# Neighbourhood attention in a hybrid encoder layer: each column group's values loaded once and kept, and the first latent head loaded in two halves

## Chip, cores and metric

The kernel runs on one core of a Trainium2 chip. The metric is the device time of one execution in microseconds (us). The parts of the core are TensorE (PE in the tables; PEld is its weight load), VectorE (DVE), ScalarE (ACT), GpSimd (POOL), and SyncE (SP), from which every DMA of this kernel is issued, in one order that is fixed when the program is built. Sixteen DMA engines serve that one queue. 1 KB is 1024 bytes here, 1 MB is 10^6 bytes.

## The reference, cut to what matters

One encoder layer over 2048 tokens of width 1024. Its first half projects the normed input into three branches, norms each 64-wide group of the joined result and projects it back; its second half is a SwiGLU feed-forward. Two of the branches matter here.

```
# A: neighbourhood attention on a 32 x 64 token grid, 4 heads of 64 channels, window 8 rows x 16 columns
s = einsum('brqhd,brjwhd->bhrqjw', qg, k_band) * dh ** -0.5
s = where(col_ok, s + bias, -inf)
p = softmax(s over the window)
o = einsum('bhrqjw,brjwhd->brqhd', p, v_band)
# B: latent attention, 8 heads, keys of 64 + 32 channels, over all 2048 tokens
s = einsum('bqhd,bkhd->bhqk', q_nope, k_nope) + einsum('bqhr,bkr->bhqk', q_rope, k_rope)
o = einsum('bhqk,bkhd->bqhd', softmax(s * scale), v)
```

## The kernel before

Stages follow one another: the projections (which write queries, keys and values to DRAM scratch), the neighbourhood attention, the latent attention, the output projection, and the feed-forward. The change is in the neighbourhood attention and at its seam with the latent attention.

**Units.** The token grid is cut into four rows of units (r = 0 to 3, eight grid rows each) and four column groups (cg = 0 to 3, sixteen grid columns each). One such group, written (r,cg), has 128 queries; a unit is one head of a group, so there are 64 units, taken as r, then cg, then head h. The keys of group (r,cg) are the grid rows of `RWIN[r]` (11, 15, 15 and 12 rows) by the columns of `CWIN[cg]` (24, 32, 32 and 24 columns).

A unit goes through three steps. `scores` (L911): two matmuls of 264 to 480 columns into the bank `sp`, then on VectorE one instruction that adds the bias and takes the maximum (L922), on ScalarE the exponential (L925), and a scaling by the reciprocal sum, on VectorE for even heads and on GpSimd for odd ones (L928). `flip` (L935): three or four transposes on TensorE into `tp`, copied to `pt` by ScalarE. `values` (L949), for two heads at once: 12 or 16 matmuls of `pt` with the value tile into `op`, copied to `ot`; after the fourth column group `ot` is stored to `mixT` (L963). There are two banks each of `sp`, `tp` and `op`.

**Loads of a group.** `load_unit` (L889) is called while the group before it is at its second head. It loads the queries `nq` (two DMAs of 128 KB, three buffers), the values `nvt` (four DMAs, one for each grid row modulo four, three buffers), and, where the table is not there yet, the bias `bt` (one buffer for each kind of column group: left edge, middle, right edge). Values of overlapping row windows are loaded again in each row of units.

**The seam.** The last units share TensorE and VectorE with the first maximum steps of the latent attention (`max_step`, L848): sixteen of them, each two matmuls into `ps` from the tiles `qh` and `kh` of latent head 0, and a reduction of 1024 columns on VectorE (L857). A latent head has five tiles: `qh`, `ql`, `kh`, `kl` of 128 x 2048 floats, and `vt` of 128 x 16 x 64 floats, together 4.72 MB, filled by eleven DMAs of `load_head` (L817). The maxima and the first half of each score need `qh` and `kh`, the second half of a score `ql` and `kl`, and the sum over values `vt`. The heads have two pools, `hda` and `hdb`, used in turn.

**What sets the order.** Within the neighbourhood stage only SP's order is written by hand, and a DMA whose data or buffers are free early may be moved ahead; the other engines are ordered by the build's scheduler. From the latent attention on, all orders are by hand. `load_head(1)` is called at the third slot of the first latent unit (L1259); since the pool `hdb` is opened inside the neighbourhood stage, on the other side of memory, its buffers are free at once, and the scheduler puts its DMAs between the loads of groups (2,0) and (2,1). A DMA on SP waits until its buffer is free and until the DMA eight places before it has landed. What is behind it in SP's order waits too.

Of the kernel before, what the change touches and what calls it, by code (L numbers as in the profile page):

```python
# [13 lines left out]
F32 = mybir.dt.float32  # L14
F32R = mybir.dt.float32r
# [9 lines left out]
P = 128  # L25
T = 2048
# [5 lines left out]
HD = 64  # L32
NAH = 4
MH = 8
NOPE = 64
ROPE = 32
# [6 lines left out]
GW = 64  # L43
# [20 lines left out]
RWIN = [(0, 11), (4, 15), (12, 15), (20, 12)]  # L64
# [14 lines left out]
def encoder_trunk(ctx: ExitStack, tc: tile.TileContext, x, cols, pos, inv, rg, ind, sel, b_ada, w_ada, w_adat, crow, w_in, w_conv3,  # L79
# [731 lines left out]
    with ExitStack() as c3:  # L811
# [2 lines left out]
        hds = [mk3("hda", 1, side="right")]  # L814
        heads = {}

        def load_head(h):  # L817


            hd = hds[h % 2]  # L820
            q1 = hd.tile([P, T], F32R, name="qh")
            q2 = hd.tile([P, T], F32R, name="ql")
            k1 = hd.tile([P, T], F32R, name="kh")
            k2 = hd.tile([P, T], F32R, name="kl")
            vt = hd.tile([P, T // P, HD], F32, name="vt")
            ns, rs = slice(h * NOPE, (h + 1) * NOPE), slice(h * ROPE, (h + 1) * ROPE)
            for t, parts in ((q1, (qnh[ns], qrh[rs], qrl[rs])), (k1, (knh[ns], krh[:ROPE], krh[:ROPE])),
                             (q2, (qnh[ns], qnl[ns])), (k2, (knl[ns], knh[ns]))):
                r = 0
                for ap in parts:  # L830
                    n = ap.shape[0]
                    dma(t[r:r + n].bitcast(F32), ap)
                    r += n
            dma(vt, vd[:, h * HD:(h + 1) * HD].rearrange("(t p) d -> p t d", p=P))
            heads[h] = [q1, q2, k1, k2, vt, None]

        def load_rest(h, q3):

# [26 lines left out]
        with ExitStack() as c2:  # L865
# [1 line left out]
            nkp = [mk("nkh", 1), mk("nkl", 1)]  # L867
            nbp = mk("nbp", 1)
            nqp = mk("nqp", 3)
            nvp = mk("nvp", 3)  # L870
            nw = mk("nw", 3)
            nsm = mk("nsm", 6)
            nop = mk("nop", 1)
# [15 lines left out]
            def load_unit(r, cg):  # L889
                r0, nr = RWIN[r]  # L890
                c0, wc = CWIN[cg]
                nq = nqp.tile([P, NAH, P], F32R, name="nq")
                for e in range(2):
                    dma(nq[e * HD:(e + 1) * HD].bitcast(F32), heads_of((nqh, nql)[e], r * CH + cg * P, P))
                nqs[(r, cg)] = nq
                vt = nvp.tile([P, 4, NAH * HD], F32, name="nvt")
                rows = nvt.rearrange("(r q) d -> q r d", q=GW)[c0:c0 + wc]
                for e in range(4):
                    n = len(range(e, nr, 4))
                    dma(vt[e * wc:(e + 1) * wc, :n], rows[:, r0 + e:r0 + nr:4])  # L900
                vts[(r, cg)] = vt
                load_bias((RCAT[r], CCAT[cg]))

            def load_bias(key):
                if key not in bias:
# [43 lines left out]
            def values(r, cg, hp, pair):  # L949

                kt = kts(r, cg)
                op = pso.tile([P, CH], F32, name="op")
                for j, (o, n) in enumerate(kt):
                    for e, pt in enumerate(pair):
                        h = 2 * hp + e
                        pe.matmul(op[e * HD:(e + 1) * HD, :P], vts[(r, cg)][:n, j, h * HD:(h + 1) * HD], pt[:n, j],
                                  start=j == 0, stop=j == len(kt) - 1, skip_group_check=True)
                if cg == 0:
                    ots[hp] = nop.tile([P, CH], F32, name=f"ot{hp}")
                s.activation(ots[hp].rearrange("p (r q) -> p r q", q=GW)[:, :, cg * 16:(cg + 1) * 16],  # L960
                             op[:, :P].rearrange("p (r q) -> p r q", q=16), AF.Copy)
                if cg == 3:
                    dma(mixT[hp * P:(hp + 1) * P, r * CH:(r + 1) * CH], ots[hp])  # L963
# [6 lines left out]
            with tc.manual_schedule(engines={ET.SP}):  # L970
# [12 lines left out]
                for i in range(len(units) + S2):  # L983
                    if M0 <= i < M0 + 16:
                        u, j = mla[(i - M0) // 8], (i - M0) % 8
                        if j == 0:
                            mxs[u] = new_max()
                        max_step(*u, j, mxs[u])
                    if i < len(units):
                        r, cg, h = units[i]  # L990
                        with tc.issue_after(last_store[0].ins):
                            if h == 1 and 12 <= i + 4 < len(units):
                                load_unit(*units[i + 4][:2])
                            if (r, h) == (0, 0) and 1 <= cg < 3:
                                load_keys(1, cg + 1)
                            if (r, cg, h) == (2, 0, 0):
                                load_head(0)
                        prs[i] = scores(*units[i])
                    if 0 <= i - S1 < len(units):
                        pts[i - S1] = flip(*units[i - S1], prs.pop(i - S1))  # L1000
                    w = i - S2
                    if 0 <= w < len(units) and w % 2:
                        r, cg, h = units[w]
                        values(r, cg, h // 2, (pts.pop(w - 1), pts.pop(w)))
                hds.append(mk3("hdb", 1, side="right"))


        mk = mk3
        tTa = mk4("tTa", 1)
        small = mk4("small3", 4)  # L1010
# [942 lines left out]
```

## Time and profile before

| | us |
|---|---|
| median of 3 runs | 3072.84 (3072.07 to 3074.15) |
| the profiled execution, its own time | 3066.38 |
| span of its trace | 3064.6 |
| neighbourhood stage, first score matmul to first latent exponential | 634.0 to 789.1 |

A row of a timeline has the start, the duration, the engine, the line, the operation, what it writes and reads, and in brackets how long the engine was idle before it and who ended the wait. A row of windows gives, for each engine, its busy time and its instructions in the stretch, then the clock granted to TensorE as a share of full speed, the mean busy share of the DMA engines, and what they moved in GB/s. The stage is five per cent of the span; where an engine waits in it, the time of the whole program follows, since the stages around it depend on it.

### The profile page before, as it was taken

To read this page: it belongs to the slowest core of one execution; us is meant where nothing else is said; L and a number is where in the kernel's file an instruction comes from. 1 tells how busy PE (TensorE), PEld (TensorE's weight loads), DVE (VectorE), ACT (ScalarE), POOL (GpSimd) and SP (SyncE) were. 2 spreads that over 40 slices of the span, in tenths; PEclk is the share of its full clock that TensorE was granted. 3 is DMA by queue.
4 is the path that set the end of the run, shared out by engine and by line. 5 is a ranking of instruction groups with operands and counts; after the bars stand their busy time and mean duration, and the time that the engine had idled before them with its cause. 6 is when DMAs were issued, how large, how long until landed. Compare 5 with 4: busy or idle time off the path is not lost. (4 is left out here: it accounts for less than half of the span.)

```text
span 3064.6 us, 39020 instructions
## 1 busy us (share of the span) xinstructions
PE 2911.2 (95%) x13554; PEld 2159.4 (70%) x13554; DVE 1978.0 (65%) x2872; ACT 1305.8 (43%) x2302; POOL 1431.0 (47%) x1043
## 2 busy tenths in 40 slices
PE   6988999978999999999999899999999999999998
PEld 5877888855555555555477688788767788888887
DVE  7778684625566666666667865565576655555556
ACT  4544444545444444444546433333444333333443
POOL 4433333422477777766655644344353544443002
PEclk9999999978999999999999999999999999999999
DMA  6566656698243354540364434344566533333566
GB/s 220 174 225 217 213 169 176 199 224 186 57 119 100 99 136 116 131 99 13 97 219 164 131 114 131 105 135 147 169 200 227 184 104 103 103 103 101 190 222 224
DMA packets 333707, 463.00 MB, mean 151 GB/s; under 512 B 40499, under 2 KB 179683, under 8 KB 328965
## 3 DMA queue, kind: packets, MB, share of 16 engines
q1 hardware_dynamic: 333510, 460.52, 49.7%
q8 instruction: 106, 1.74, 0.2%
q14 instruction: 91, 0.75, 0.1%
HBM read 338.58 MB, written 117.51 MB: 149 GB/s over the span
## 5 line engine op out<-in xcount | busy, mean ns | idle before, releaser
L857 DVE TENSOR_REDUCE mx<-ps 128x1 f32<-128x1024 f32 x256 | 313.3, 1224 | 236.7 <-PE ps L856 236.5
L1361 DVE TENSOR_TENSOR whl<-draw,whl 128x512 fp32r<-128x512 f32 x372 | 311.3, 872 | 182.1 <-ACT whl L1360 181.7
L1230 ACT ACTIVATE p<-st 128x1024 f32<-128x1024 f32 x256 | 262.1, 1024 | 361.6 <-PE st L1223 271.3
L1360 ACT ACTIVATE whl<-draw 128x512 fp32r<-128x512 f32 x372 | 219.9, 625 | 307.6 <-PE bk L1466 214.0
L1237 POOL TENSOR_TENSOR acc<-acc,p 128x512 f32<-128x512 f32 x192 | 275.4, 1434 | 44.1 <-ACT p L1230 39.1
L1465 PE MATMUL bk<-whl 128*128 128x512 f32 x616 | 243.7, 396 | 18.2 <-DVE whl L1361 17.9
L1168 PE MATMUL op<-p,vt 128*64 128x512 f32 x1024 | 249.6, 608 | 0.0
L1464 PE MATMUL bk<-whl 128*128 128x512 f32 x616 | 240.8, 391 | 3.4 <-ACT whl L1360 3.4
L1466 PE MATMUL bk<-whl 128*128 128x512 f32 x616 | 240.5, 390 | 0.0
L1386 POOL TENSOR_TENSOR t<-draw 128x512 f32<-128x512 f32 x88 | 122.2, 1389 | 233.9 <-DMA draw<-in_w_gu 192.0
L1400 ACT ACTIVATE whl<-t 128x512 fp32r<-128x512 f32 x176 | 111.0, 631 | 278.2 <-PE bk L1682 236.1
L1680 PE MATMUL bk<-q,whl 128*128 128x512 f32 x528 | 209.0, 396 | 13.1 <-ACT ev L1687 8.8
L1681 PE MATMUL bk<-q,whl 128*128 128x512 f32 x528 | 207.3, 393 | 0.0
L1222 PE MATMUL st<-qh,kh 128*128 128x512 f32 x512 | 205.7, 402 | 1.2 <-ACT p L1230 1.2
L1682 PE MATMUL bk<-q,whl 128*128 128x512 f32 x528 | 206.7, 391 | 0.0
L1401 DVE TENSOR_TENSOR whl<-t,whl 128x512 fp32r<-128x512 f32 x176 | 164.4, 935 | 61.4 <-ACT whl L1400 56.9
L262 POOL TENSOR_TENSOR wlo<-raw,whi 128x768 fp32r<-128x768 f32 (+4 forms) x59 | 112.8, 1913 | 193.7 <-ACT whi L261 184.4
L1223 PE MATMUL st<-ql,kl 128*128 128x512 f32 x512 | 201.1, 393 | 0.0
L1386 POOL TENSOR_TENSOR t<-draw,t 128x512 f32<-128x512 f32 x88 | 118.4, 1346 | 137.0 <-DMA draw<-in_w_gu 117.5
L856 PE MATMUL ps<-kh,qh 96*128 96x512 f32 x512 | 176.5, 426 | 5.9 <-DMA kh<-krh 4.0
L320 PE MATMUL mm<-whi,hh 128*128 128x288 f32 (+3 forms) x512 | 170.2, 344 | 8.1 <-ACT hh L384 4.9
L856 PEld LDWEIGHTS ps<-kh,qh 96*128 96x128 f32 x512 | 87.1, 191 | 115.2 <-DVE acc L1238 79.5
(370 smaller groups left out, 7243.6 us busy)
## 6 DMA issues: line engine op xcount, KB each, us to landing
draw<-in_w_gu SPq DMA_DIRECT2D x176, 256.0 KB
draw<-actd SPq DMA_DIRECT2D x70, 512.0 KB
actd<-xs SPq DMA_DIRECT2D x88, 256.0 KB
draw<-wdt SPq DMA_DIRECT2D x40, 512.0 KB
actd<-ev SPq DMA_DIRECT2D x66, 256.0 KB
wt<-in_w_adat SPq DMA_DIRECT2D x32, 512.0 KB
draw<-in_w_out SPq DMA_DIRECT2D x32, 512.0 KB
draw<-in_w_down SPq DMA_DIRECT2D x30, 512.0 KB
```

The source lines that it names most:

```text
L856: pe.matmul(ps[:, e], qs, kh[:QKD, kc:kc + CH], start=True, stop=True)
L857: v.reduce_max(mx[:, t, i:i + 1], ps.rearrange("p a b -> p (a b)"), axis=AX.X)
L1168: pe.matmul(tl["op"][e * HD:(e + 1) * HD], vt[:, 2 * kp + e], tl["p"][kp][:, e], start=kp == 0, stop=kp == NP - 1, skip_group_check=True)
L1230: s.activation(p, st, AF.Exp, scale=SC)
L1237: g.tensor_tensor(out=acc[:, 0], in0=a[:, 0], in1=p[kp][:, 0], op=ALU.add)
L1360: s.activation(w[:, 0], raw[:, e], AF.Copy)
L1361: v.tensor_tensor(out=w[:, 1], in0=raw[:, e], in1=w[:, 0].bitcast(F32), op=ALU.subtract)
L1386: g.tensor_tensor(out=t, in0=a, in1=b, op=op)
L1464: pe.matmul(ps, th, wh, start=first, stop=False, skip_group_check=True)
L1465: pe.matmul(ps, th, wl, start=False, stop=False, skip_group_check=True)
L1466: pe.matmul(ps, tl, wh, start=False, stop=last, skip_group_check=True)
L1680: pe.matmul(ps, w[:, 0, k], th, start=first and k == 0, stop=False, skip_group_check=True)
```

## The change

The value tiles become four, one for each column group, each with all 32 grid rows (eight blocks of four), and are kept through the stage. `load_unit` fills blocks 0 to 2 of a group in the first row of units, blocks 3 to 7 in the second, and nothing in the third and fourth. The matmuls of `values` read block `RWIN[r][0] // 4 + j` instead of block j.

`load_head` gets a `parts` argument. Part 0 allocates all five tiles and loads `qh` and `kh`; part 1 loads `ql`, `kl` and `vt`. Head 0 is loaded as part 0 with unit (2,0,0), and as part 1 with unit (3,2,0). The pool `hdb` is opened after the neighbourhood stage's pools are closed, not before.

```diff
-        def load_head(h):
+        def load_head(h, parts=(0, 1)):
...
             hd = hds[h % 2]
+            if 0 in parts:
+                q1, q2, k1, k2 = [hd.tile([P, T], F32R, name=n) for n in ("qh", "ql", "kh", "kl")]
+                heads[h] = [q1, q2, k1, k2, hd.tile([P, T // P, HD], F32, name="vt"), None]
+                fill(q1, qnh[ns], qrh[rs], qrl[rs])
+                fill(k1, knh[ns], krh[:ROPE], krh[:ROPE])
+            if 1 in parts:
+                q1, q2, k1, k2, vt, _ = heads[h]
+                fill(q2, qnh[ns], qnl[ns])
+                fill(k2, knl[ns], knh[ns])
+                dma(vt, vd[:, h * HD:(h + 1) * HD].rearrange("(t p) d -> p t d", p=P))
...
-            nvp = mk("nvp", 3)
+            nvp = mk("nvp", 1)
...
-                vt = nvp.tile([P, 4, NAH * HD], F32, name="nvt")
+                if r < 2:
+                    load_values(r, cg)
+                load_bias((RCAT[r], CCAT[cg]))
+
+            def load_values(part, cg):
+
+                c0, wc = CWIN[cg]
+                if part == 0:
+                    vts[cg] = nvp.tile([P, T // GW // 4, NAH * HD], F32, name=f"nvt{cg}")
+                b0, b1 = ((0, 3), (3, T // GW // 4))[part]
                 rows = nvt.rearrange("(r q) d -> q r d", q=GW)[c0:c0 + wc]
                 for e in range(4):
-                    n = len(range(e, nr, 4))
-                    dma(vt[e * wc:(e + 1) * wc, :n], rows[:, r0 + e:r0 + nr:4])
-                vts[(r, cg)] = vt
-                load_bias((RCAT[r], CCAT[cg]))
+                    dma(vts[cg][e * wc:(e + 1) * wc, b0:b1], rows[:, 4 * b0 + e:4 * b1:4])
...
-                            if (r, cg, h) == (2, 0, 0):
-                                load_head(0)
+                            if (r, cg, h) in ((2, 0, 0), (3, 2, 0)):
+                                load_head(0, (r - 2,))
...
-                hds.append(mk3("hdb", 1, side="right"))
-
-
+
+
+        hds.append(mk3("hdb", 1, side="right"))
```

The lines below move by four to ten (L894 becomes L898, L900 becomes L912, L908 becomes L918, L832 becomes L826, L963 becomes L973, L919 becomes L929, L956 becomes L966).

SP's order before, from the last values of group (2,0) to the queries of group (2,1); the tiles `qh` to `vt` in it are those of latent head 1:

```order
L900 DMA nvt<-nvt 24x3x256
L832 DMA qh<-qnh 64x2048
L832 DMA qh<-qrh 32x2048
L832 DMA qh<-qrl 32x2048
L832 DMA kh<-knh 64x2048
L832 DMA kh<-krh 32x2048 x2
L832 DMA ql<-qnh 64x2048
L832 DMA ql<-qnl 64x2048
L832 DMA kl<-knl 64x2048
L832 DMA kl<-knh 64x2048
L834 DMA vt<-vd 128x16x64
L894 DMA nq<-nqh 64x4x128
```

SP's order in the changed kernel, from the queries of group (2,0) to those of (2,1) and the stores of row 1; `qh` and `kh` here are those of head 0:

```order
L898 DMA nq<-nqh 64x4x128
L898 DMA nq<-nql 64x4x128
L826 DMA qh<-qnh 64x2048
L826 DMA qh<-qrh 32x2048
L826 DMA qh<-qrl 32x2048
L826 DMA kh<-knh 64x2048
L826 DMA kh<-krh 32x2048 x2
L898 DMA nq<-nqh 64x4x128
L898 DMA nq<-nql 64x4x128
L973 DMA mixT<-ot_7123 128x512
L973 DMA mixT<-ot_7172 128x512
```

In front of the queries of (2,1) there stand now the six DMAs of head 0's first half (2.10 MB) where the eleven of head 1 stood (4.72 MB). Head 0's own eleven stood earlier in the kernel before, between the queries of (0,3) and the values of (1,3). Head 1's eleven are now behind the last `mixT` store of the stage and the four row stores `q3s<-mr` of the latent attention.

SP's order before, from the stores of row 2 to the bias of group (3,3):

```order
L963 DMA mixT<-ot_7564 128x512
L963 DMA mixT<-ot_7613 128x512
L894 DMA nq<-nqh 64x4x128
L894 DMA nq<-nql 64x4x128
L900 DMA nvt<-nvt 32x3x256 x4
L894 DMA nq<-nqh 64x4x128
L894 DMA nq<-nql 64x4x128
L900 DMA nvt<-nvt 24x3x256 x4
L908 DMA bt_8097<-in_nbias 128x1152
L843 DMA q3s<-qrh 32x2048 x2
```

The same place in the changed kernel, with `ql`, `kl` and `vt` of head 0:

```order
L973 DMA mixT<-ot_7540 128x512
L973 DMA mixT<-ot_7589 128x512
L898 DMA nq<-nqh 64x4x128
L898 DMA nq<-nql 64x4x128
L826 DMA ql<-qnh 64x2048
L826 DMA ql<-qnl 64x2048
L826 DMA kl<-knl 64x2048
L826 DMA kl<-knh 64x2048
L839 DMA vt<-vd 128x16x64
L898 DMA nq<-nqh 64x4x128
L898 DMA nq<-nql 64x4x128
L918 DMA bt_8053<-in_nbias 128x1152
```

Five DMAs (2.62 MB) stand between the queries of (3,2) and those of (3,3), and the eight value loads there are gone.

TensorE's order before, the last scores of the stage to the first latent score; the four `sp` rows of 288 columns are group (3,3), and the `mi` rows transpose the first two maxima:

```order
L919 MATMUL sp<-nk,nq 128x288 x4
L939 MATMUL tp<-ident,sb 128x128 x3
L956 MATMUL op<-pt,nvt 64x128 x6
L939 MATMUL tp<-ident,sb 128x128 x6
L956 MATMUL op<-pt,nvt 64x128 x6
L939 MATMUL tp<-ident,sb 128x128 x3
L919 MATMUL sp<-nk,nq 128x288 x2
L956 MATMUL op<-pt,nvt 64x128
L919 MATMUL sp<-nk,nq 128x288 x2
L939 MATMUL tp<-ident,sb 96x128 x3
L956 MATMUL op<-pt,nvt 64x128 x5
```

The same place in the changed kernel:

```order
L860 MATMUL ps<-kh,qh 128x512 x2
L966 MATMUL op<-pt,nvt_6605 64x128 x6
L929 MATMUL sp<-nk,nq 128x288 x8
L949 MATMUL tp<-ident,sb 96x128 x3
L1167 MATMUL mi<-ident,m_8315 4x128
L949 MATMUL tp<-ident,sb 96x128 x6
L966 MATMUL op<-pt,nvt_6776 64x128
L1167 MATMUL mi<-ident,m_8323 4x128
L949 MATMUL tp<-ident,sb 96x128 x3
L966 MATMUL op<-pt,nvt_6776 64x128 x11
L1232 MATMUL st<-qh,kh 128x512
```

All four scores of (3,3) come now after everything of the groups before it, and after the last maximum step; no other work of TensorE stands between them. Earlier in the stage the sixteen maximum steps begin after the third score of group (2,0), where they began behind the fourth before.

## Rows read from the trace of the kernel before

**Rows 1.** The page: busy time and share of the span by engine; DMA by slices.

```profile
PE 2911.2 (95%) x13554; PEld 2159.4 (70%) x13554; DVE 1978.0 (65%) x2872; ACT 1305.8 (43%) x2302; POOL 1431.0 (47%) x1043
...
DMA  6566656698243354540364434344566533333566
```

**Rows 2.** Windows: busy time by engine, granted clock, DMA share, GB/s.

```profile
629.00:740.00 111.00, 86.53 (x504) 58.91 (x503) 43.88 (x147) 53.08 (x174) 25.34 (x21) 0.79 1.02 221
...
655.00:674.00 19.00, 13.28 (x91) 9.31 (x91) 3.35 (x16) 7.42 (x29) 3.05 (x3) 0.78 1.07 208
...
733.10:763.90 30.80, 30.76 (x206) 21.70 (x207) 23.66 (x69) 20.03 (x65) 10.75 (x8) 0.93 0.52 152
...
896.00:900.00 4.00, 4.00 (x20) 1.83 (x18) 2.55 (x3) 1.02 (x1) 3.92 (x4) 1.00 1.01 211
```

**Rows 3.** Timeline of VectorE: first bias instruction of (0,3), (1,0), (1,3), (3,3).

```profile
661.70 0.43 DVE L922 CUSTOM_DVE_ANT_0 sb<-sp,bt 128x264 f32<-128x264 f32 x1 [6.42 <-DMA bt<-in_nbias]
...
673.59 0.53 DVE L922 CUSTOM_DVE_ANT_0 sb<-sp,bt 128x360 f32<-128x360 f32 x1 [7.26 <-DMA bt<-in_nbias]
...
704.87 0.53 DVE L922 CUSTOM_DVE_ANT_0 sb<-sp,bt 128x360 f32<-128x360 f32 x1 [5.77 <-DMA bt<-in_nbias]
...
776.01 0.46 DVE L922 CUSTOM_DVE_ANT_0 sb<-sp,bt 128x288 f32<-128x288 f32 x1 [1.03 <-DMA bt<-in_nbias]
```

**Rows 4.** Timeline of TensorE: scores of (0,3), first maximum step, scores of (2,1).

```profile
655.02 0.48 PE L919 MATMUL sp<-nk,nq 128*128 128x264 f32 x2 [0.98 <-DMA nq<-nql]
...
718.49 1.19 PE L856 MATMUL ps<-kh,qh 96*128 96x512 f32 x2 [3.98 <-DMA kh<-krh]
...
733.14 1.94 PE L919 MATMUL sp<-nk,nq 128*128 128x480 f32 x4 [2.23 <-DMA nq<-nql]
```

**Rows 5.** DMA issues of 600 to 800 us: count, KB of each.

```profile
nq<-nqh SPq DMA_DIRECT2D x16, 128.0 KB
...
mixT<-ot SPq DMA_DIRECT2D x8, 256.0 KB
...
bt<-in_nbias SPq DMA_DIRECT2D x2, 720.0 KB
...
bt<-in_nbias SPq DMA_DIRECT2D x2, 576.0 KB
bt<-in_nbias SPq DMA_DIRECT2D x2, 528.0 KB
...
bt<-in_nbias SPq DMA_DIRECT2D x1, 960.0 KB
```

**Rows 6.** Timeline of SP: queries of (2,1); first load after the scores of (3,3).

```profile
717.18 11.15 SPq L894 DMA_DIRECT2D nq<-nqh  x1
728.37 0.62 SPq L894 DMA_DIRECT2D nq<-nql  x1
...
779.05 0.79 SPq L843 DMA_DIRECT2D q3s<-qrh  x2
```

**Rows 7.** Groups of TensorE in 733.1 to 763.9 us: count, busy us, mean ns, idle before.

```profile
L919 PE MATMUL sp<-nk,nq 128*128 128x480 f32 (+3 forms) x36 | 11.4, 427 | 2.2 <-DMA nq<-nql 2.2
L956 PE MATMUL op<-pt,nvt 128*64 128x128 f32 (+2 forms) x96 | 9.8, 284 | 0.0
L939 PE MATMUL tp<-ident,sb 128*96 128x128 f32 (+2 forms) x56 | 9.0, 279 | 0.0
L856 PE MATMUL ps<-kh,qh 96*128 96x512 f32 x18 | 6.6, 449 | 0.0
```

**Rows 8.** Timeline of ScalarE: last copy of row 2; first exponential of the latent attention.

```profile
763.92 0.26 ACT L960 ACTIVATE ot<-op 128x128 f32<-128x128 f32 x1
...
789.11 1.02 ACT L1230 ACTIVATE p<-st 128x1024 f32<-128x1024 f32 x1 [4.01 <-PE st L1218]
```

**Rows 9.** Timeline of SP in the latent attention, behind the load of head 2.

```profile
900.81 13.11 SPq L843 DMA_DIRECT2D q3s<-qrh  x2
...
919.58 0.50 SPq L1178 DMA_DIRECT2D o<-o  x1
```

More of the change, by code (lines that the diff above doesn't have):

```diff
@@ L815, in encoder_trunk, with fill @@
         heads = {}
-        def load_head(h):
[L820 to L825, printed above, removed]
+        def load_head(h, parts=(0, 1)):
             ns, rs = slice(h * NOPE, (h + 1) * NOPE), slice(h * ROPE, (h + 1) * ROPE)
-            for t, parts in ((q1, (qnh[ns], qrh[rs], qrl[rs])), (k1, (knh[ns], krh[:ROPE], krh[:ROPE])),
-                             (q2, (qnh[ns], qnl[ns])), (k2, (knl[ns], knh[ns]))):
+            def fill(t, *aps):
                 r = 0
-                for ap in parts:
+                for ap in aps:
                     n = ap.shape[0]
@@ L833, in load_head @@
                     r += n
-            dma(vt, vd[:, h * HD:(h + 1) * HD].rearrange("(t p) d -> p t d", p=P))
-            heads[h] = [q1, q2, k1, k2, vt, None]
+            hd = hds[h % 2]
+            if 0 in parts:
[8 more added lines that the diff above has]
+                dma(vt, vd[:, h * HD:(h + 1) * HD].rearrange("(t p) d -> p t d", p=P))
         def load_rest(h, q3):
@@ L955, in values @@
                         h = 2 * hp + e
-                        pe.matmul(op[e * HD:(e + 1) * HD, :P], vts[(r, cg)][:n, j, h * HD:(h + 1) * HD], pt[:n, j],
+                        pe.matmul(op[e * HD:(e + 1) * HD, :P], vts[cg][:n, RWIN[r][0] // 4 + j, h * HD:(h + 1) * HD], pt[:n, j],
                                   start=j == 0, stop=j == len(kt) - 1, skip_group_check=True)
```

## Prediction

> **What bounds the kernel now.** The page says TensorE, with 95% of the span, but its DMA line has one place at 9 and 8 tenths, the ninth and tenth of the 40 slices [rows 1]: the neighbourhood stage. The windows come next. From 629 to 740 us the DMA engines are busy all the time (share 1.02) at 221 GB/s, while TensorE has work for 86.5 of 111 us, at a granted clock of 0.79 [rows 2]. So that part is bound by transfers, and the timelines say by which. VectorE begins groups (0,3), (1,0) and (1,3) when a bias table lands, after waits of 6.42, 7.26 and 5.77 us [rows 3]; TensorE begins (0,3) and (2,1) when queries land, and the first maximum step when `kh` lands, after 3.98 us [rows 4]. From 733 us on nothing but 2.2 us of waiting for queries is left idle on TensorE [rows 7]: the rest of the stage is bound by compute.
>
> Does one queue at a steady rate explain these landings? From 661.70 to 673.59 us [rows 3] the order has the queries of (1,0), the second half of `qh`, half of `kh`, and the values and bias of (1,0): 0.26 + 0.52 + 0.52 + 0.37 + 0.74 = 2.42 MB in 11.89 us, 203 GB/s. From there to 704.87 us the same count gives 7.53 MB in 31.28 us, 241 GB/s. So yes, a load lands when what stands before it has been moved, at 203 to 241; I take 215, near the windows' 208 to 221 [rows 2]. Sizes are those of the issues [rows 5] or of the shapes in the orders.
>
> **What is removed and moved.** Values: before, 53 rows of units' windows times 112 columns of 1 KB are 6.08 MB; now 32 rows times 112 are 3.67 MB. In the second row of units it is more than before (20 grid rows instead of 15). Head 0 (4.72 MB) goes from the first and second row of units to the third and fourth; head 1 (4.72 MB) from the third row into the latent attention.
>
> *To the first maximum step.* TensorE begins (0,3) at 655.02 us, when its queries land [rows 4]; the queue up to there is the same but for 0.09 MB. Behind it stand now, to the bias of (0,3): 0.30 + 0.54 MB; to that of (1,0): 0.26 + 0.49 + 0.74; to that of (1,1): 0.26 + 0.66 + 0.98; to that of (1,3): the stores of row 0, two pairs of queries, two value loads and the bias, 0.52 + 0.52 + 1.15 + 0.74. Together 7.16 MB, at 215 GB/s 33.3 us: (1,3) begins at 688.3 instead of 704.87 us. Then the queries of (2,0) and head 0's first half, 2.36 MB, 11.0 us: `kh` lands at 699.3 us. The changed order has the first maximum step after the third score of (2,0), so TensorE stops there until then. Its own work from 688.3 on (ten score matmuls, 16 transposes, 32 value matmuls, by the prices below 7.6 us) is done sooner. I take 700 us.
>
> *To the end of row 2.* The mean prices of 733.1 to 763.9 us [rows 7] are 0.317 us for a score matmul, 0.102 for a value matmul, 0.161 for a transpose, 0.367 for a maximum matmul; they add to 36.8 us in a stretch of 30.8, so each counts 0.837. That stretch begins with the scores of (2,1) and ends with the last copy of row 2 at 763.92 us [rows 8]. Counted in the changed order from the first maximum step to the same place: 38, 160, 78 and 22, so (12.0 + 16.3 + 12.6 + 8.1) x 0.837 = 41.0 us. Row 2 ends at 741 us, 23 us earlier than before.
>
> *Where part is given back.* In SP's order the second half of head 0 stands behind the stores of row 2, which wait for that copy, and in front of the queries and bias of (3,3). From 741 us the queue has the second store, the queries of (3,2), 2.62 MB of `ql`, `kl`, `vt`, the queries of (3,3) and its bias: 0.26 + 0.26 + 2.62 + 0.26 + 0.59 = 4.0 MB, 18.6 us. To this comes what the same pattern cost before: behind head 1's `vt` the issue of the queries of (2,1) took 11.15 us, and after the second half of them was issued at 728.99 it was 733.14 until TensorE had them [rows 6, 4], 4 us in which the queue ran nearly empty. So the bias lands at 763.6 us. TensorE's own work to that point (12, 72, 30 and 10, by the same prices 16.4 us) ends at 757.4 us, and the new order leaves it nothing else to do: some 6 us are lost. Bounds for this hold: 0, if the transfers go at 241 GB/s and the 4 us don't recur; 11 us at 203 GB/s with the wait of 4 us counted twice. I take the middle.
>
> *The seam.* Before, the bias of (3,3) came at 776.01 us, SP's first load behind that group's scores left at 779.05, and the first exponential of the latent attention ran at 789.11 [rows 3, 6, 8]. The 10.1 us from SP's load remain, less half a microsecond, since the `q3s` row stores now stand ahead of the `mixT` stores; the 3.0 us become about 1.8, as the four scores come without others' work between. 763.6 + 1.8 + 9.6 = 775.0 us, against 789.1: 14.1 us saved.
>
> *Head 1 in the latent attention* I cost at nothing. What hides it: the DMA engines have nothing else there (the eleventh to eighteenth slices stand at 2 to 5 tenths, [rows 1]), and head 2's load, the same eleven DMAs, ran beside TensorE at 4.00 of 4 us busy at full clock [rows 2]; SP was held 13.11 us behind it, and a copy of an output left only at 919.58 [rows 9]. Head 1's maxima are wanted two latent units later. Behind SP's hold stand the second `q3s` load and the copy of the first unit's output, due some 25 us after the first exponential; 4.72 MB need 22 us. Without this cover the price is those 22 us. The `hdb` buffers now overlap the stage's own, but SP reaches them behind the stage's last store anyway.
>
> A rule of the Trainium skill would put the hold at nothing: "DMA: Bandwidth & Descriptors", section "Bandwidth", wants transfers of 1 MiB or more for three quarters of the peak and measures 341 GB/s at that size. By 341 GB/s the 4.0 MB would take 11.7 us, below TensorE's 16.4 us. No row here agrees: with head 2's pieces of half a megabyte and 8 KB rows the windows show 211 GB/s. That figure would give the time of the second case below.
>
> **The sum.** 3066.38 of the profiled execution less 14.1 is 3052.3 us; the median of the runs is 6.46 us above that execution, so 3072.84 less 14.1, 3058.7 us. With 241 GB/s and the 4 us it saves 7 us more (4.8 up to `kh`, 2 in the hold), with 203 GB/s and a hold of 11 us it saves 7 us less: 3052 to 3066.
>
> **The rivals.**
> 1. *Likeliest, 3058.7 us:* as above.
> 2. *No hold at (3,3), 3047 us.* At 241 GB/s `kh` lands at 694.5, row 2 ends at 735.5, and without the 4 us the bias of (3,3) comes with TensorE's work at 752; first exponential at 763.5, 25.6 us saved. For it: 241 GB/s was measured over 31 us. Against: 203 to 211 elsewhere, and the wait behind `vt`.
> 3. *The gain is swallowed, 3069 us.* At 203 GB/s the first maximum step comes at 702; if TensorE gets the clock of 0.79 of the first part instead of the 0.93 of the priced stretch [rows 2], 41 us become 48, row 2 ends at 750, the bias lands at 774 and the exponential comes at 785: 4 us saved. For it: new idle places in front of (1,0), (1,1), the first maximum step and (3,3), and clocks of 0.78 where such waits were [rows 2]. Against: these waits are shorter than before.
> 4. *Slower, 3081 us.* Head 1's load stands in the path: the first latent units need something that SP issues behind it. Then 22 us come back, and 3058.7 + 22 = 3081. It decides as soon as more than 14 of the 22 us are exposed. For it: SP is held up to 13 us at such a place. Against: the row stores and `k3` of the first two units are ahead of it in the order.
>
> **How the numbers follow.** Chances: 0.54, 0.22, 0.16, 0.08. About 0.2% (6.1 us) is what a measurement of this kernel can tell from no change. The first two are faster, and a quarter of the third: 0.80; the rest of the third is the same: 0.12; the fourth is slower: 0.08. The range goes from below the second to the third: 3046 to 3070.
>
> **What would show it.** Right: the bias of (1,3) lands near 688 us, the first maximum step waits for `kh` until about 700, row 2's last copy is near 741, VectorE waits for the bias of (3,3) until about 764 behind an idle TensorE, the first latent exponential is near 775, and from there on everything is shifted by the same 14 us; head 1's load then shows DMA at about 1.0 for 22 us with TensorE full. Wrong: a (1,3) start after 700, an (3,3) start without a DMA wait, or idle places of TensorE in the first four latent units.

## The result and the profile after

| | before | after |
|---|---|---|
| median us | 3072.45 (3070.99 to 3074.15) | 3054.64 (3051.29 to 3060.38) |
| ratio, 95% interval | 1 | 0.9944 [0.9927, 0.9961] |
| profiled execution, its span | 3066.38, 3064.6 | 3055.07, 3053.3 |
| T, see below | 154.5 | 140.4 |

The change made the kernel faster by 17.8 us; the interval is 12 to 22 us. The forecast was 14.1. Two executions further below, one of head1_pad (11071.73 us) and one of pad_spread (12784.67 us), lie far outside all others and are left out of every ratio.

One correction first. Some passages ahead of this section give SP's loads to the wrong latent head. In the kernel before, the eleven DMAs between the queries of (2,0) and (2,1) are head 0's: the first maximum step reads the tiles that they fill. The eleven spread between the queries of (0,3) and the values of (1,3) are head 1's. Both heads have 4.72 MB, so no sum changes; but what left the first two rows of units is head 1, the load that nothing needs there, and head 0 was not moved to the third row: its first half stayed in front of (2,1), and only its second half went, to the fourth row.

T in the table is the time from the first bias instruction of the neighbourhood stage to the first exponential of the latent attention, each in its own profiled execution. It leaves out how the stages before and behind vary from run to run, so it is used below beside the ratios. How far T itself varies is said at after_again.

The page of the kernel after, busy time and DMA by slices:

```profile
PE 2903.2 (95%) x13554; PEld 2154.3 (71%) x13554; DVE 1984.1 (65%) x2872; ACT 1304.9 (43%) x2302; POOL 1429.3 (47%) x1043
...
DMA  6566655695554345440364434344566533333566
```

A slice is 76 us long. Against [rows 1] the tenth slice has 5 instead of 8 and the eleventh 5 instead of 2: transfers have moved out of the neighbourhood stage into the latent attention. The windows of the kernel after (columns as in [rows 2]; a granted clock of 1.00 is the upper of TensorE's two levels, 2.4 GHz, 0.50 the lower, 1.2 GHz, and a value between them is a mean over the window):

```profile
629.00:740.00 111.00, 96.45 (x648) 66.88 (x649) 57.28 (x192) 66.07 (x225) 32.60 (x27) 0.89 0.70 165
655.00:674.00 19.00, 13.33 (x89) 9.32 (x89) 5.00 (x24) 7.85 (x31) 2.97 (x3) 0.82 1.10 210
700.00:741.00 41.00, 39.44 (x274) 27.28 (x273) 26.10 (x71) 24.15 (x83) 11.51 (x9) 0.88 0.27 81
741.00:764.00 23.00, 19.44 (x152) 13.69 (x150) 15.12 (x39) 12.91 (x37) 6.05 (x5) 0.99 0.78 173
764.00:775.00 11.00, 8.71 (x47) 6.28 (x48) 4.16 (x19) 4.75 (x14) 2.01 (x2) 0.56 0.46 121
775.00:800.00 25.00, 24.36 (x107) 13.24 (x107) 15.46 (x17) 9.54 (x11) 9.86 (x8) 1.00 0.92 201
```

In the same 111 us TensorE did 648 matmuls instead of 504 [rows 2]. Up to about 700 us the queue is still full; from 700 to 741 it is nearly empty and TensorE works; from 741 to 775 TensorE has a hole again. The last row is head 1's load: DMA at 0.92 beside a TensorE that is busy for 24.36 of 25 us.

VectorE's first bias instructions of (0,3), (1,0), (1,3) and (3,3), as in [rows 3], with that of the first unit ahead of them:

```profile
636.51 0.43 DVE L932 CUSTOM_DVE_ANT_0 sb<-sp,bt 128x264 f32<-128x264 f32 x1
...
663.35 0.43 DVE L932 CUSTOM_DVE_ANT_0 sb<-sp,bt 128x264 f32<-128x264 f32 x1 [8.63 <-PE tp L949]
...
671.51 0.53 DVE L932 CUSTOM_DVE_ANT_0 sb<-sp,bt 128x360 f32<-128x360 f32 x1 [3.77 <-DMA bt<-in_nbias]
...
692.08 0.53 DVE L932 CUSTOM_DVE_ANT_0 sb<-sp,bt 128x360 f32<-128x360 f32 x1 [3.19 <-DMA bt<-in_nbias]
...
766.39 0.46 DVE L932 CUSTOM_DVE_ANT_0 sb<-sp,bt 128x288 f32<-128x288 f32 x1 [5.41 <-DMA bt<-in_nbias]
```

TensorE at the scores of (0,3), the first maximum step and the scores of (3,3), as in [rows 4]; ScalarE at row 2's last copy and at the first latent exponential, as in [rows 8]:

```profile
659.27 0.78 PE L929 MATMUL sp<-nk,nq 128*128 128x264 f32 x2 [5.79 <-DMA nq<-nql]
...
701.96 1.15 PE L860 MATMUL ps<-kh,qh 96*128 96x512 f32 x2 [1.56 <-DMA kh<-krh]
...
744.66 0.27 ACT L970 ACTIVATE ot<-op 128x128 f32<-128x128 f32 x1
...
765.18 1.30 PE L929 MATMUL sp<-nk,nq 128*128 128x288 f32 x4 [4.62 <-DMA nq<-nql]
...
776.94 1.02 ACT L1240 ACTIVATE p<-st 128x1024 f32<-128x1024 f32 x1 [1.79 <-PE st L1228]
```

From the bias of (0,3) on, each stretch is shorter up to row 2's end (19 us earlier than in [rows 8]); then TensorE idles 4.62 us and VectorE 5.41 us in front of (3,3), and the first exponential is 12.2 us earlier than before. SP shows two holds, behind the `vt` of head 0's second half and behind that of head 1:

```profile
749.93 10.63 SPq L898 DMA_DIRECT2D nq<-nqh  x1
760.61 0.62 SPq L898 DMA_DIRECT2D nq<-nql  x1
...
787.76 12.15 SPq L847 DMA_DIRECT2D q3s<-qrh  x2
800.46 0.50 SPq L1188 DMA_DIRECT2D o<-o  x1
```

The same output copies left at 814.75, 837.30 and 882.41 us before, and at 800.46, 823.02 and 868.12 after: 14.3 us earlier, three times. A copy near the end of the latent attention came 13.0 us earlier (1508.04 instead of 1521.05), the end of these two spans 11.3; single runs of one kernel lie up to 13 us apart (3047.56 to 3060.14 for the same kernel below), so the 17.8 of the medians and the 14.3 of the traces do not contradict each other.

### The profile page after: what moved, and what is told of

It is laid out like the page before. It is cut to its first block, busy times and chain, and to the rows that moved or that the text cites. A ratio compares the mean times of both kernels' runs of the same rounds, so it can differ in the third digit from the quotient of the medians.

```text
span 3053.3 us, 38974 instructions
## 1 busy us (share of the span) xinstructions
PE 2903.2 (95%) x13554; PEld 2154.3 (71%) x13554; DVE 1984.1 (65%) x2872; ACT 1304.9 (43%) x2302; POOL 1429.3 (47%) x1043
## 5 line engine op out<-in xcount | busy, mean ns | idle before, releaser
L1247 POOL TENSOR_TENSOR acc<-acc,p 128x512 f32<-128x512 f32 x192 | 276.6, 1440 | 43.0 <-ACT p L1240 38.1
L321 PE MATMUL mm<-wlo,hh 128*128 128x288 f32 (+3 forms) x512 | 165.5, 335 | 2.5 <-DVE wlo L262 1.3
```

Source lines behind the costliest of these rows:

```text
L1247: g.tensor_tensor(out=acc[:, 0], in0=a[:, 0], in1=p[kp][:, 0], op=ALU.add)
```

## The experiments

All times are ratios to the kernel before, with 95% intervals. No kernel leaves work out. S is the last part of T, from row 2's last copy on ScalarE to the first latent exponential, in us; the hold at (3,3) falls into it.

| run | second half of head 0 | values | head 1's load | ratio | T | S |
|---|---|---|---|---|---|---|
| before | with the first at (2,0) | reloaded | in the stage | 1 | 154.5 | 25.2 |
| after | (3,2) | kept | behind it | 0.9944 [0.9927, 0.9961] | 140.4 | 32.3 |
| after_again | (3,2) | kept | behind it | 0.9942 [0.9928, 0.9955] | 141.3 | 31.4 |
| split_only | (3,2) | reloaded | in the stage | 1.0013 [1.0001, 1.0025] | 160.7 | 34.8 |
| head1_pad | (2,0) | reloaded | behind it | 0.9928 [0.9915, 0.9940] | 134.9 | 25.3 |
| pad_split | (3,2) | reloaded | behind it | 0.9926 [0.9912, 0.9940] | 136.0 | 34.7 |
| values_whole | (2,0) | kept | behind it | 0.9922 [0.9906, 0.9937] | 139.3 | 22.9 |
| half2_early | (2,2) | kept | behind it | 0.9913 [0.9898, 0.9928] | 137.0 | 23.7 |
| half2_late | behind the loads of (3,3) | kept | behind it | 0.9928 [0.9915, 0.9940] | 135.1 | 28.1 |
| spread | pieces at (2,2), (2,3), (3,0) | kept | behind it | 0.9908 [0.9895, 0.9921] | 132.7 | 24.8 |
| spread_again | the same | kept | behind it | 0.9912 [0.9898, 0.9927] | 132.8 | 25.1 |
| pad_spread | the same | reloaded | behind it | 0.9919 [0.9901, 0.9937] | 125.4 | 26.0 |
| spread_parts | the same | kept, eight tiles | behind it | 0.9897 [0.9883, 0.9912] | 131.5 | 25.0 |
| head1_twice | (3,2) | kept | behind it, twice | 0.9969 [0.9955, 0.9983] | 136.3 | 31.4 |

**The same kernel again** (after_again): 

> The changed kernel once more, as the measure for the other runs of this series. Both theories: 14 to 18 us faster than before (ratio 0.9942 to 0.9955). The landmarks of its trace move together with the start of the stage by some us: the first maximum step about 65 us after the first bias instruction, the first latent exponential about 140 us after it, as in the first profile.

It repeats the ratio to 0.0002 and T to 0.8 us. That is not all that T can vary: head1_twice (below) differs from the changed kernel only behind the stage, and SP's order in the stage is the same, yet its T is 4.1 and 5.0 us shorter than in these two. It gains them between the first maximum step and row 2's last copy: 38.1 us, where both others took 42.7. TensorE has hardly any idle time there in either, but not the same clock. The window from 702 to 714 us in after and in head1_twice, and the two ends of the stretch in head1_twice:

```profile
702.00:714.00 12.00, 12.00 (x57) 7.72 (x57) 5.33 (x13) 4.12 (x13) 1.18 (x1) 0.57 0.07 24
```

```profile
702.00:714.00 12.00, 12.00 (x88) 8.16 (x88) 7.80 (x24) 7.52 (x26) 3.85 (x3) 0.98 0.17 50
...
704.38 0.63 PE L867 MATMUL ps<-kh,qh 96*128 96x512 f32 x2
...
742.51 0.26 ACT L977 ACTIVATE ot<-op 128x128 f32<-128x128 f32 x1
```

So a difference of T of up to some 5 us between two kernels is not read as theirs. S lies closer together in these three, 31.4 to 32.3 us. All kernels with the hold at (3,3) have an S of 31.4 to 34.8, all others one of 22.9 to 28.1.

**Which part gains: head 1's place alone** (head1_pad). The kernel before, with the `hdb` line moved and a tile of 20 KB per partition added to the stage that nothing uses:

```diff
+            padp = mk("padp", 1)
+            pad = padp.tile([P, 5 * 1024], F32, name="pad")
+            g.memset(pad[:, :1], 0.0)
...
-                hds.append(mk3("hdb", 1, side="right"))
...
+        hds.append(mk3("hdb", 1, side="right"))
```

> The kernel before with its value loads and its undivided head 0; only a pad of 20 KB per partition is added in the stage, so that the buffers of latent head 1 overlap it and head 1's eleven DMAs fall behind the stage. Theory of the queue (a load lands when what stands ahead of it has moved at about 215 GB/s): 4.72 MB leave the queue ahead of the first maximum step, which comes at about 700 us instead of 718; the queries of (2,1) still stand behind all of head 0 and land at about 717 instead of 733; nothing holds (3,3); the first latent exponential is some 16 us earlier, so 12 to 17 us faster than before, all but the same as the changed kernel. Theory of the values (the gain is the 2.4 MB and 32 DMAs of values saved): no more than 4 us faster.

The moved line alone gives word for word the order of the kernel before (it was not run). With the tile, the stage's memory reaches `hdb`, and head 1 goes behind the stage: SP issues its first DMA at 771.07 us. Nothing else is changed, values are reloaded, head 0 stands whole at (2,0), and the ratio is as good as the changed kernel's. The first maximum step comes 64.0 us after the first bias instruction, where it came after 83.9 before. TensorE at the first maximum step and at (2,1), VectorE at (3,3), ScalarE at the first exponential, in head1_pad:

```profile
700.54 0.73 PE L856 MATMUL ps<-kh,qh 96*128 96x512 f32 x2 [2.96 <-DMA kh<-krh]
...
715.64 1.97 PE L922 MATMUL sp<-nk,nq 128*128 128x480 f32 x4 [3.45 <-DMA nq<-nql]
...
758.58 0.46 DVE L925 CUSTOM_DVE_ANT_0 sb<-sp,bt 128x288 f32<-128x288 f32 x1 [1.26 <-PE tp L942]
...
771.50 1.02 ACT L1233 ACTIVATE p<-st 128x1024 f32<-128x1024 f32 x1 [4.07 <-PE st L1221]
```

The hold is here in front of (2,1), 3.45 us, as before, and there is none at (3,3). So it is head 1's 4.72 MB leaving the queue ahead of the first maximum step that gains.

**The split alone** (split_only). The kernel before with head 0 split as in the change, the `hdb` line moved, no tile added: head 1 stays early. 

> The kernel before with head 0 in two halves alone: the values are loaded again in each row of units, and head 1's DMAs stay early in the stage. Queue: up to the first maximum step nothing changes (718 us); the queries of (2,1) land 12 us earlier than before, 720 instead of 733 us; from there the hold at (3,3) takes 6 us back or more, since a value load stands there too: 3 to 7 us faster. Values: 0 faster.

Wrong: it is not faster. By the ratio it is 4 us slower (0.13%; the interval only just leaves out no change), and T is 6.2 us longer. TensorE at the first maximum step and VectorE at (3,3):

```profile
724.25 1.19 PE L860 MATMUL ps<-kh,qh 96*128 96x512 f32 x2 [3.92 <-DMA nvt<-nvt]
...
786.38 0.46 DVE L926 CUSTOM_DVE_ANT_0 sb<-sp,bt 128x288 f32<-128x288 f32 x1 [4.82 <-DMA bt<-in_nbias]
```

The first maximum step is no earlier than in [rows 4], since head 1's load is still ahead of it; (2,1) began at 729.81 us instead of 734.42, and that is lost at (3,3), where the same hold appears as in the changed kernel (S is 9.6 us longer than before). Why (1,3) began 4.5 us later than before against the stage's start is open.

**Without kept values** (pad_split): head1_pad's tile, and head 0 split as in the change. 

> The kernel before with head 0 in two halves and the pad that puts head 1 behind the stage; only the kept values are missing against the changed kernel. Queue: first maximum step at about 700 us, the queries of (2,1) at about 702, a hold of 6 to 8 us before (3,3) as in the changed kernel: 12 to 16 us faster than before, within 2 us of the changed kernel. Values: it lacks what brings the gain, so 0 to 5 us faster.

It has the changed kernel's hold, 5.47 us at (3,3), and is no slower than the changed kernel: T is 4.4 us shorter, within what T varies by, and the ratios' intervals overlap. Fewer bytes for the values show no gain here. VectorE at (3,3) in pad_split:

```profile
762.49 0.46 DVE L929 CUSTOM_DVE_ANT_0 sb<-sp,bt 128x288 f32<-128x288 f32 x1 [5.47 <-DMA bt<-in_nbias]
```

**Where the second half stands.** The changed kernel with one line edited:

```diff
-                            if (r, cg, h) in ((2, 0, 0), (3, 2, 0)):
-                                load_head(0, (r - 2,))
+                            if (r, cg, h) == (2, 0, 0):                       # values_whole
+                                load_head(0)
...
+                            if (r, cg, h) in ((2, 0, 0), (2, 2, 0)):          # half2_early
+                                load_head(0, (cg // 2,))
...
+                            if (r, cg, h) in ((2, 0, 0), (3, 2, 2)):          # half2_late
+                                load_head(0, (r - 2,))
```

values_whole: 

> The changed kernel with head 0 loaded whole at (2,0), as before; the values are kept and head 1 is behind the stage. Queue: the first maximum step as in the changed kernel (about 702 us in its profile), the queries of (2,1) land 12 to 15 us behind it, at 715; TensorE has maximum steps and the work of (2,0) until then; nothing holds (3,3). The two stalls are of like size, so within 4 us of the changed kernel, 12 to 19 us faster than before. Rival (the split itself brings the gain): less than half the gain, under 8 us faster.

half2_early: 

> The changed kernel with head 0's second half at (2,2) instead of (3,2), where the DMA engines are at a share of 0.27. Queue theory: the queries of (2,3) now stand behind the 2.62 MB, which wait in turn for the stores of row 1, so TensorE waits for them some 5 us near 730 us and the hold only changes its place: within 3 us of the changed kernel. Rival (idle DMA time is enough to hide a transfer): no wait for queries or bias from 705 us on, and 5 to 7 us faster than the changed kernel.

half2_late: 

> The changed kernel with head 0's second half behind the loads of (3,3) instead of ahead of them. Queue: the bias of (3,3) lands before its turn, near 753 us, and VectorE no longer waits for it; `ql`, `kl` and `vt` land at about 767, and the loads of the seam behind them, so the first latent exponential comes at 772 to 775 instead of 777: 2 to 5 us faster than the changed kernel. Rival (the second half only moves its wait to the first latent score): the exponential not before 777, the same time as the changed kernel.

All three are free of the wait at (3,3). values_whole gains it (S 22.9) and pays ahead of (2,1), so T is nearly the changed kernel's: SP issues those queries only at 716.92 us, and though TensorE shows no wait for them, it has only maximum steps and the work of (1,3) and (2,0) left and does them at a clock of 0.50 from 706 to 718 us. From the first maximum step to row 2's last copy 48.4 us pass there, 42.7 in the changed kernel. What lowered the clock is not shown. half2_early came out between its two expectations: a wait of 1.66 us for the queries of (2,3), not 5, stands in place of the hold. So most of the hold is not moved but gone, which fits with the row of units ahead of it having an empty queue (0.27 in the window from 700 to 741 us above). In half2_late, as expected, (3,3) no longer waits and begins at 755.22 us; the first latent unit waits 2.32 us for a row store instead. TensorE in half2_early at (2,3), and in half2_late at the first latent score:

```profile
735.40 1.10 PE L929 MATMUL sp<-nk,nq 128*128 128x360 f32 x4 [1.66 <-DMA nq<-nql]
```

```profile
769.79 1.66 PE L1228 MATMUL st<-q3s,k 33*128 33x512 f32 x3 [2.32 <-DMA q3s<-mr]
```

**The pieces spread** (spread, spread_again): `ql` with (2,2), `kl` with (2,3), `vt` with (3,0).

```diff
-                            if (r, cg, h) in ((2, 0, 0), (3, 2, 0)):
-                                load_head(0, (r - 2,))
+                            if h == 0 and (r, cg) in ((2, 0), (2, 2), (2, 3), (3, 0)):
+                                load_head(0, (((2, 0), (2, 2), (2, 3), (3, 0)).index((r, cg)),))
```

> The changed kernel with head 0's second half in three pieces: `ql` at (2,2), `kl` at (2,3), `vt` at (3,0). Queue: each piece is 1.05 MB (5 us) or 0.52 MB with the wait behind its short rows, less than the time of a group (6 us), so no group waits for queries or bias by more than 1 us from 705 us on; the hold of 5 to 6 us is gone: 4 to 7 us faster than the changed kernel, 19 to 24 us faster than before. Rival (pieces cost the same as the whole): as the changed kernel.

> spread once more, on the same chip as pad_spread. If its gain over the changed kernel is real: ratio to before 0.989 to 0.993, first latent exponential 132 to 135 us after the first bias instruction, no wait for a DMA on TensorE or VectorE after the one for kh.

Both runs agree: T is 8 us shorter than the changed kernel's, and the intervals of their ratios end at 0.9921 and 0.9927, where the changed kernel's begin (0.9927 and 0.9928). spread_again's one wait for a DMA behind `kh`, 0.23 us, is outside what was expected of it, and nothing. ScalarE at row 2's last copy and at the first latent exponential in spread, VectorE at (3,3) between them, and the windows of spread around it:

```profile
746.24 0.27 ACT L972 ACTIVATE ot<-op 128x128 f32<-128x128 f32 x1
...
757.46 0.43 DVE L934 CUSTOM_DVE_ANT_0 sb<-sp,bt 128x288 f32<-128x288 f32 x1
...
771.03 1.02 ACT L1242 ACTIVATE p<-st 128x1024 f32<-128x1024 f32 x1 [1.77 <-PE st L1230]
```

```profile
700.00:741.00 41.00, 39.58 (x283) 27.42 (x280) 26.44 (x74) 24.48 (x82) 10.68 (x8) 0.88 0.67 154
741.00:764.00 23.00, 22.92 (x176) 16.61 (x174) 18.46 (x56) 16.37 (x51) 8.00 (x7) 1.00 0.32 96
```

No wait stands at (3,3) any more, TensorE is full from 741 to 764 us (22.92 against 19.44 us above), and the transfers lie in the stretch ahead, where nobody waits for them. What the hold cost is read from S, since up to row 2's last copy spread and the changed kernel take the same time (107.9 and 108.2 us from the first bias instruction): 31.4 to 32.3 us with it, 24.8 and 25.1 without, so 6.3 to 7.5 us, the 4.62 us of idle time and the low clock behind it.

**Head 1 issued twice** (head1_twice): at its place in the latent attention all eleven DMAs once more.

```diff
                         load_head(1)
+                        load_head(1, (2,))
```

> The changed kernel with every DMA of head 1 issued twice at the start of the latent attention, into the same tiles with the same data: 4.72 MB more. Forecast's view (such a load is hidden there): SP is held about 22 us longer, the first unit's output copy leaves near 823 instead of 800 us, the rows of maxima for the third unit some 15 us late; these have slack, so 0 to 5 us slower than the changed kernel. Rival 4 of the prediction (the load stands in the path of the first latent units): 22 us slower than the changed kernel, which is as slow as before or slower.

Between the two: about 8 us slower than the changed kernel (0.9969 against 0.9944, intervals that overlap a little). From the first exponential to the fourth output copy it takes 9.7 us longer (100.9 against 91.2). The windows of head1_twice, and TensorE and SP in them:

```profile
775.00:800.00 25.00, 25.00 (x112) 14.04 (x111) 15.57 (x18) 9.82 (x10) 10.91 (x9) 1.00 1.03 211
800.00:819.00 19.00, 16.74 (x75) 8.76 (x71) 12.85 (x15) 7.13 (x8) 6.31 (x5) 1.00 1.04 212
819.00:831.00 12.00, 7.01 (x21) 3.21 (x22) 1.29 (x2) 1.99 (x3) 6.18 (x5) 0.72 0.42 86
```

```profile
823.99 1.40 PE L1235 MATMUL st<-q3s,k 33*128 33x512 f32 x4 [7.25 <-DMA q3s<-mr]
```

```profile
807.49 11.74 SPq L854 DMA_DIRECT2D q3s<-qrh  x2
819.32 0.50 SPq L1195 DMA_DIRECT2D o<-o  x1
819.92 1.44 SPq L1179 DMA_DIRECT2D q3s<-mr  x2
```

One load of 22 us is hidden; of a second one TensorE sees 7.25 us, when the row stores of the next unit stand behind it. The slack at this place, an estimate from 22 less 9.7, is thus some 12 us beyond one load, and rival 4's price was never near.

**Are kept values worth anything once the hold is gone?** (pad_spread): spread with reloaded values and the unused tile. 

> The four pieces of head 0 as in spread, but each unit's values are loaded anew as before; a tile of 20 KB per partition that nothing uses keeps head 1 behind the stage. Against spread: 2.41 MB more pass the queue in the stage, most of them in the third and fourth row of units. Theory (head 1's place is the gain, kept values are worth nothing by themselves): within 5 us of spread, first latent exponential 131 to 136 us after the first bias instruction (spread 132.66). Rival (kept values are worth the time of their bytes): 2.41 MB at 215 GB/s, 11 us later than spread, waits for queries or bias in the third or fourth row.

The rival, 11 us later, is wrong: T is 7 us shorter than spread's, which is below the theory's range too. The ratios do not rank the two (five runs of pad_spread: 3037.85, 3038.09, 3048.07, 3050.24 and 3050.48 us; spread's ten: 3038.54 to 3048.57). Of the 7.4 us against spread_again, 5.5 lie between the first maximum step and row 2's last copy, and there the clock differs. The window from 702 to 714 us in spread_again and in pad_spread:

```profile
702.00:714.00 12.00, 12.00 (x59) 7.48 (x58) 5.49 (x14) 4.88 (x16) 1.50 (x2) 0.58 0.07 24
```

```profile
702.00:714.00 12.00, 12.00 (x92) 8.59 (x90) 10.12 (x29) 9.17 (x29) 4.55 (x3) 1.00 0.95 223
```

That part is of the size by which T varies for one and the same stage, so it is not put down to the values. Another 2.8 us are gained before the first maximum step, and 0.9 are given back in S. Why should reloading begin sooner? The waits of SP from 600 to 640 us in the kernel after (what waited for what, us in total, times, longest) and its rows around the first value load:

```profile
SPq L912 <- PE mm L536: 4.7, 1, 4.7
```

```profile
621.03 9.46 SPq L668 DMA_DIRECT2D vd<-vt  x4
635.03 1.57 SPq L912 DMA_DIRECT2D nvt<-nvt  x4
```

SP waits there for the last matmul of the projections, and all that it has to load waits behind. The kernels that reload show 0.6 us of it at most. Of pad_spread:

```profile
622.40 9.36 SPq L668 DMA_DIRECT2D vd<-vt  x4
631.87 1.25 SPq L909 DMA_DIRECT2D nvt<-nvt  x3
```

By the built program's addresses, the kept tile of the first column group (8 KB per partition) reaches 4 KB over the operand tiles `hh` that those matmuls read, among them the one that is read last. A tile of 4 KB at the same place reaches only 192 bytes over the one of them that is done with first.

**The kept tiles cut in two** (spread_parts): spread, with 3 and 5 blocks in tiles of their own.

```diff
-                if part == 0:
-                    vts[cg] = nvp.tile([P, T // GW // 4, NAH * HD], F32, name=f"nvt{cg}")
                 b0, b1 = ((0, 3), (3, T // GW // 4))[part]
+                vt = nvp.tile([P, b1 - b0, NAH * HD], F32, name=f"nvt{cg}p{part}")
+                vts.setdefault(cg, []).extend((vt, j) for j in range(b1 - b0))
...
+                    vt, jb = vts[cg][RWIN[r][0] // 4 + j]
```

> spread, with each column group's kept values in two tiles (3 and 5 blocks) instead of one of 8. In the kernels with kept values SP's first value load waited 4.7 us for the last matmuls of the projection stage (after: 635.03 us, where before and the kernels that reload had it at 629 to 632, right behind the store of the latent values). By their addresses, the kept tile of the first column group lies over the projection's operand tiles hh, and the smaller first tile no longer does; that of the second still does. Theory (this wait, and not the bytes, starts the stage late): the first value load follows the store of the latent values within 1 us, the queries of (0,2) and what follows land 2 to 4 us earlier against the first bias instruction, first latent exponential 128.5 to 131 us after it (spread 132.7), ratio 0.989 to 0.991. Rival (the second load meets the same wait, or the queue is the bound later anyway): the first bias of (1,3) stays 55 to 55.5 us behind the first bias instruction as in spread, no gain.

SP in spread_parts:

```profile
621.29 9.22 SPq L668 DMA_DIRECT2D vd<-vt  x4
630.57 1.69 SPq L914 DMA_DIRECT2D nvt0p<-nvt  x4
632.30 0.59 SPq L900 DMA_DIRECT2D nq<-nqh  x1
632.93 0.61 SPq L900 DMA_DIRECT2D nq<-nql  x1
634.93 1.73 SPq L914 DMA_DIRECT2D nvt1p<-nvt  x4
```

The overlap was the cause of the wait: the first load follows the store at once. The second group's tile, which still lies over `hh`, waits until 634.93 us, so the gain is smaller than expected: (1,3) begins 53.7 us behind the first bias instruction (55.4 in spread, 48.1 in pad_spread), T is 1.3 us shorter. The mechanism is shown, its worth is not: 1.3 us is below what T resolves. By its ratio, 0.9897, spread_parts is the fastest of all, 15 us ahead of the changed kernel by the medians; against spread the intervals overlap.

## Why the prediction was right, point by point

*The bound.* Right: one queue, filled in order, set every landing up to the first maximum step. From the queries of (0,3) to the bias of (1,3) the 33.3 us forecast for 7.16 MB were 692.08 - 659.27 = 32.8 us, 218 GB/s.

*The start of that stretch.* Here a step failed: "the queue up to there is the same but for 0.09 MB". The queries of (0,3) landed 4.25 us later than in [rows 4], 1.9 of it because the stage itself began later in this execution, much of the rest by SP's wait of 4.7 us in front of the kept tiles' first load (spread_parts, with 1.5 us of that wait, has 1.4 us less from the first bias instruction to these queries). So (1,3) came 3.8 us later than forecast. The order of the DMAs was read, their waits for memory were not.

*To row 2's end.* The first maximum step waited for `kh` and ran at 701.96 us (700 forecast). From there to row 2's last copy 42.7 us were measured and 41.0 forecast: the window from 700 to 741 us had a clock of 0.88 where the prices came from a stretch with 0.93 [rows 2]. The forecast of this stretch stands on the clock: at 0.98 instead of 0.57 behind the first maximum step the same stage took 38.1 us (head1_twice).

*The hold at (3,3).* Right in place and cause: SP held 10.63 us behind `vt`, TensorE idle, the bias of (3,3) last (766.39, forecast 763.6; 21.7 us after row 2's end against 22.6). Its price was a little low: 6 us, where removing it shortened S by 6.3 to 7.5. The idle TensorE also came back at a clock of 0.56 in the window from 764 to 775 us, which the sum did not have.

*The seam.* From that bias to the first exponential 10.5 us, 11.4 forecast. The exponential came at 776.94 us, forecast 775.0.

*Head 1 in the latent attention.* Right: no stop of TensorE, and twice the load was needed to make one.

*The sum.* 14.1 us by the steps, 14.3 by the three output copies, 14.1 by T. Counted from the stage's first bias instruction, no landmark is off by more than 2 us: (1,3) +1.9, the first maximum step 0, row 2's end +1.8, (3,3) +0.9, the first exponential 0. That the last is exact is luck: the slower clock cancels with a hold and a seam that were each 0.9 us shorter than forecast, and T of one stage varies by 5 us.

*What was right for a wrong reason.* The prediction counted 2.4 MB fewer of values among what is saved, and held that the overlap of the `hdb` buffers with the stage's own changes nothing, since SP reaches head 1 behind the stage's last store anyway. The runs say otherwise. Without that overlap head 1 stays early, moved line or not (split_only). No run shows that kept values save time by their bytes: in the first two rows of units, where the queue is the bound, they load more than before (32 rows of the grid instead of 26, 0.7 MB, an estimate of 3 us at 218 GB/s), and they start later. What they do is take 20 KB more of each partition, and that alone sends head 1 behind the stage (head1_pad). Of the rivals, the second (no hold) is what spread became. Of the third only a part came, the low clock behind the first maximum step; for the fourth the runs show nothing.

## What to carry to other kernels

Before a load is made smaller, ask which loads stand ahead of the one that is waited for, and whether each is needed there: here 4.72 MB that nobody wanted for a hundred microseconds cost more than all the bytes saved. Where a scheduler hoists whatever finds its buffer free, the size and address of an unrelated tile set the order of transfers; a larger tile can hold a prefetch back, and can also make the first load of the next stage wait for the last reader of the stage before. Put a prefetch into the stretch whose window shows an empty queue and a full TensorE, in pieces, and not ahead of the last loads of a stage.

## What the runs showed of the hardware that was not expected

- SP's next issue behind a load of `vt` (128 x 16 pieces of 256 bytes) was held for 9.05 us (after_again) to 13.11 us [rows 9] wherever `vt` stood at the end of an unbroken run of a head's DMAs and the next issue followed at once (10.63 and 12.15 us in after), but for 8.00 us in spread and 3.42 us in pad_spread, where `vt` went alone with (3,0). The prediction took such a hold as a price of `vt`; these numbers speak for a part of it coming from what stands before `vt` in the queue, which no run isolates.
- TensorE came out of a stop of 4.62 us at a granted clock of 0.56 in the window from 764 to 775 us, which begins 1.2 us before the stop ends, and out of one of 7.25 us at 0.72 over a window of 12 us that includes the stop. In pad_spread, where waits in the second row of units are shorter, the clock from 655 to 700 us was 1.00 instead of 0.89 in spread_again, and from 702 to 714 us 1.00 instead of 0.58. That may be most of why T there is 7 us shorter; no run tells it apart from the bytes.
- One and the same stage (after, after_again, head1_twice) ran with a mean clock of 0.57, 0.65 and 0.98 from 702 to 714 us, and its T varied by 5 us with it. Ahead of the low clock TensorE had waited for `kh` (1.56 us in after); in head1_twice the clock was at 0.50 from 696 to 702 us already, TensorE was still busy when `kh` landed, and no wait stands there. What decides between the two is open.
